# Transposes of attention outputs one list step later and behind the newest matmul

## The chip, the cores and the metric

The kernel runs on one core of a Trainium2 chip. The metric is the device time of one execution in microseconds. Engines are named as in the profile: PE is TensorE's matmuls and PEld its weight loads, DVE is VectorE, ACT is ScalarE, POOL is GpSimd, SP is SyncE, which issues the weight loads from memory.

## The reference

Two transformer blocks of two layers each, on 256 tokens of width 1024 (the second block also carries 256 context tokens in its first layer). Every layer is `h = h + mixer(norm(h)) @ w_out` followed by a gated convolutional feed-forward layer (inner width 2816). The four mixers are the four attentions of the change:

```
layer 1: 8 heads with dilated causal patterns, 8 heads with forget-gate bias, head width 64
layer 2: 8 heads of differential attention, value width 128, RMS norm of each head's output
layer 3: gated linear recurrence, and 8 heads of window attention with a sink column, for the
         256 tokens (keys: context and tokens) and for the context tokens (keys: context)
layer 4: 8 heads of global attention over context and tokens, 8 heads of neighbourhood attention
o = softmax(scores) @ v ;  out = concat(heads) @ w_out ;  h = h + out
```

## The kernel before, in words

All matrix products are split in three: each float32 operand is cut into a high and a low part (`split`, L636), and a product is high x high, high x low and low x high, three matmuls on the same accumulator. Weights come from memory as `raw`, and ScalarE (`wh`) and VectorE (`wl`) cut them (L496, L497).

An attention works on groups of four heads (two pairs; in layer 2 two double heads). For each head the scores are multiplied on TensorE, VectorE finds the extreme and adds the mask, ScalarE takes the exponential, TensorE transposes the probabilities (L810, L820), ScalarE copies them to SBUF, and TensorE multiplies them by the values into the PSUM tile `o`. When a pair of heads is done, `fin_half` (L826) ends it: VectorE inverts the sums and scales `o` into `on` (L832), TensorE transposes the two blocks of 128 tokens of `on` (L836), and `split` cuts the result into `mixh` and `mixl` (L639, L640; `exh`, `exl` in layer 3), which the output projection multiplies. In layer 2 the same is done by `finish` (L1094 to L1110), where the factor comes from a square sum on ScalarE and a power on GpSimd, with the scaling on L1106 and the transposes on L1109. PSUM has two buffers for scores, two for transposes of all kinds, one for `o` and three for projections; `on` has two buffers.

The work is traced as a list of steps. `weave` (L307) spreads a filler list over an attention's list: before entry k of an attention list of length A, the first ceil(k n / A) of n filler steps have been traced. Filler is the next group's projections (12 matmuls a step, or 24), and in the last group of a stage the output projection on the chunks that are ready (`p_out`, 18 matmuls a step in the first, second and last stage, 6 for the last output projection of the third). In layer 1 an attention list has 4 entries (one head each, the second and fourth with the pair's ending inside), in layer 2 6 entries (4 pieces of maps and 2 endings), in layers 3 and 4 10 entries (8 pieces of one head and 128 queries, and 2 endings). The last groups' filler lists have 13 steps (layer 1), 12 (layer 2) and 9 (layer 4); in layer 3 the two groups on the tokens share one filler list of 16. The context attention of layer 3 is woven into the feed-forward layer of layer 2, one entry about every second step.

The order in which each engine gets its instructions is not the traced one. A planner places them by a model of their times: of the instructions whose inputs the model holds ready, an engine gets the one that was traced first. On the chip every engine then works through its own instructions in that fixed order and waits where an input is late. `issue_after(x)` adds one rule to the plan: what is traced inside comes after x on x's engine (in order only; it doesn't wait for x to finish). The kernel before uses it elsewhere, behind weight cuts on VectorE (L589, L1742).

Of the kernel before, what the change touches and what calls it, by code (L numbers as in the profile page):

```python
# [17 lines left out]
S = 256  # L18
# [358 lines left out]
class Prog:  # L377
# [120 lines left out]
            self.W[key] = (h, l)  # L498

    def mm(self, o, a, b, start, stop):  # L500
        self.nc.tensor.matmul(o, a, b, start=start, stop=stop)  # L501

    def mark(self, name):
        def f():
# [318 lines left out]
        for kb in range(nkb):  # L823
            self.mm(o, pts[:, kb], v(kb), kb == 0, kb == nkb - 1)

    def fin_half(self, b, p, h, l):  # L826
        nc = self.nc
        rec = self.small.tile([128, 2, 2], F32, tag="rec", name="rec")
        hs = slice(2 * p, 2 * p + 2)
        nc.vector.reciprocal(rec, b.rs[:, :, hs])  # L830
        on = self.nat.tile([128, 2, 128], F32, tag="on", name="on", bufs=self.bufs[3])
        nc.vector.tensor_tensor(on.rearrange("p a (h d) -> p a h d", d=HD), b.o[:, :, hs],  # L832
                                rec[:, :, :, None].to_broadcast([128, 2, 2, HD]), op=ALU.mult)
        ps = self.ps_t.tile([128, S], F32, tag="t", name="tt")
        for t in range(2):
            nc.tensor.transpose(ps[:, t * 128:(t + 1) * 128], on[:, t], self.ident)  # L836
        self.split(h, l, ps)

    def x_add(self, sts=(), g=None):
        def upd(m, ps):  # L840
# [64 lines left out]
    def plan_attn0(self):  # L905
        boxes = [Box() for _ in range(4)]

        def attend(b, mask, mi, extra=None):
            steps = []

            def head(i):
                if i == 0:
                    b.o = self.ps_o.tile([128, 2, 4, HD], F32, tag="o", name="o")
                    b.rs = self.small.tile([128, 2, 4], F32, tag="rsum", name="rsum")
                p, e = i // 2, i % 2
                P = []
                for qb in range(2):
                    s = self.s_tile()
                    qs, n = slice(qb * 128, (qb + 1) * 128), 128 * (qb + 1)
                    self.qk_s(s[:, :S], (b.q[0][:, e, p, qs], b.q[1][:, e, p, qs]), (b.k[0][:, p], b.k[1][:, p]),  # L920
                              extra(i) if extra else None)
                    P.append(self.soft(s, self.C[mask][:, S - n:], n, b.rs[:, qb, i:i + 1])[0])
                self.causal_pv(P, [b.o[:, 0, i], b.o[:, 1, i]], [b.v[:, kb, i * HD:(i + 1) * HD] for kb in range(2)])
                if i % 2:
                    self.fin_half(b, p, self.mixh[mi][:, p], self.mixl[mi][:, p])
            return [((), lambda i=i: head(i)) for i in range(4)]

        def proj_a(g):
            b = boxes[g]
# [114 lines left out]
    def plan_attn1(self, st, fill, early):  # L1044
# [23 lines left out]
        def attend(g):  # L1068
# [25 lines left out]
            def finish(i):  # L1094
                nc = self.nc
                ss = self.small.tile([128, 2], F32, tag="oss", name="oss")
                v = self.small.tile([128, 2], F32, tag="osv", name="osv")
                rs = b.rs[:, 0, :, i]
                nc.vector.scalar_tensor_tensor(v, rs, 1e-5, rs, op0=ALU.mult, op1=ALU.mult)
                for qb in range(2):  # L1100
                    sq = self.nat.tile([128, 128], F32, tag="osq", name="osq", bufs=2)
                    nc.scalar.activation(sq, b.o[:, qb, i], AF.Square, accum_out=ss[:, qb:qb + 1])
                nc.vector.scalar_tensor_tensor(v, ss, 1.0 / 128, v, op0=ALU.mult, op1=ALU.add)
                r = self.pow_mhalf(v, 2)
                on = self.nat.tile([128, 2, 128], F32, tag="on", name="on", bufs=self.bufs[3])
                nc.vector.tensor_mul(on, b.o[:, :, i], r[:, :, None].to_broadcast([128, 2, 128]))  # L1106
                ps = self.ps_t.tile([128, S], F32, tag="t", name="tt")
                for qb in range(2):
                    nc.tensor.transpose(ps[:, qb * 128:(qb + 1) * 128], on[:, qb], self.ident)  # L1109
                self.split(self.mixh[g][:, i], self.mixl[g][:, i], ps, self.gsub)  # L1110
            for i in range(2):
                for qb in range(2):
                    steps.append(((), lambda i=i, qb=qb: maps(i, qb)))
                steps.append(((), lambda i=i: finish(i)))
            return steps

        self.st1 = self.stat_open(LAT, "sta")
        out = self.p_open("1", first) + fill + proj(0)
# [144 lines left out]
    def plan_even(self, s1, s2):  # L1263
# [83 lines left out]
        def attend(i, lat):  # L1347
# [29 lines left out]
            def finish(p):  # L1377
# [4 lines left out]
                dst = E.sl if lat else E.sc  # L1382
                if p == 0:
                    dst.append(ex([128, 2, S]))
                self.fin_half(b, p, dst[i][0][:, p], dst[i][1][:, p])
            for j in range(4):
                for qb in range(2):
                    steps.append(((), lambda j=j, qb=qb: one(j, qb)))
                if j % 2:
                    steps.append(((), lambda p=j // 2: finish(p)))  # L1390
            return steps

        H = [Box() for _ in range(4)]

# [330 lines left out]
    def plan_odd(self, st):  # L1725
# [51 lines left out]
        def attend(i):  # L1777
            steps, b = [], Q[i]

            def one(j, qb):  # L1780
                nc = self.nc
                if j == 0 and qb == 0:
# [24 lines left out]
            for j in range(4):  # L1807
                for qb in range(2):
                    steps.append(((), lambda j=j, qb=qb: one(j, qb)))
                if j % 2:  # L1810
                    steps.append(((), lambda p=j // 2: self.fin_half(b, p, self.mixh[i][:, p], self.mixl[i][:, p])))
            return steps

        st3 = self.stat_open(LAT, "sta")

# [82 lines left out]
```

## Time and profile before

| | |
|---|---|
| median of 3 runs | 1726.1 us (1724.31 to 1729.87) |
| the profiled execution | 1726.9 us, span 1725.1 us |
| mean granted TensorE clock | 0.981 |
| PE / PEld / DVE / ACT / POOL busy | 97 / 91 / 80 / 55 / 3% of the span |
| instructions | 31957 |

The span goes from the first to the last instruction of the profiled execution. By the tiles in the timeline, the four attention stages lie at about 20 to 131, 335 to 475, 666 to 950 (with the recurrence) and 1300 to 1546 us, the context attention between 475 and 666 us beside a feed-forward layer; the rest is feed-forward layers. A busy time is the union of an engine's instructions; matmuls overlap each other in their modelled lengths, so the start of the next one tells the pace.

### The profile page before, as it was taken

How to read it: one execution, taken by the hardware profiler on the slowest of the kernel's cores; microseconds unless marked ns; L12 is line 12 of the kernel's file. 1: busy time of each engine (PE TensorE's matmuls, PEld its weight loads, DVE VectorE, ACT ScalarE, POOL GpSimd, SP SyncE). 2: the span in 40 equal slices, each digit the busy share in tenths (PEclk: the TensorE clock that was granted, in tenths of full speed). 3: DMA queues.
4: the chain of work that ended last, by engine and by line, in shares of the span. 5: the costliest groups of instructions: out<-in, count | busy, mean ns of one | idle time of the engine just before them, and what ended most of it. 6: DMA issues, size and time to landing. Idle time of an engine off the chain costs nothing.

```text
span 1725.1 us, 31957 instructions
## 1 busy us (share of the span) xinstructions
PE 1670.7 (97%) x12336; PEld 1574.1 (91%) x12336; DVE 1371.5 (80%) x2830; ACT 945.7 (55%) x1687; POOL 59.0 (3%) x75
## 2 busy tenths in 40 slices
PE   7999999999899999999989999999998999999999
PEld 7999999999899999899978988888888998999999
DVE  6798999887787888766786888897779864479887
ACT  6666456656675768444545652342344554466554
POOL 0000000000100000100000000000000220000000
PEclk9999999999999999999989999999998999799999
DMA  8446776554456565334311555655549521135663
GB/s 305 140 142 220 231 219 210 173 173 132 125 173 194 184 206 162 123 124 133 110 62 41 181 182 165 189 169 185 181 150 315 184 62 38 62 121 165 198 191 123
DMA packets 80664, 277.97 MB, mean 161 GB/s; under 512 B 8960, under 2 KB 12160, under 8 KB 80256
## 3 DMA queue, kind: packets, MB, share of 16 engines
q1 hardware_dynamic: 79216, 273.30, 49.6%
q10 hardware_dynamic: 1296, 2.62, 0.4%
q8 instruction: 97, 1.59, 0.4%
q14 instruction: 55, 0.45, 0.1%
HBM read 274.84 MB, written 1.05 MB: 160 GB/s over the span
## 4 chain that ended last, share of the span: by engine, by line
PE 83%; DVE 10%; ACT 4%; issue 2%; DMA 0%; POOL 0%; DVEq 0%; ACTq 0%; POOLq 0%
PE acc L501 55%; PE s L501 20%; PE o L501 4%; DVE wl L497 3%; DVE junk L591 2%; PE ptp L820 2%; ACT wh L496 1%; PE tt L741 1%; DVE x L856 0%; DVE cc L1025 0%; PE stv L501 0%; PE tt L836 0%; DVE nt L1143 0%; ACT L1373 0%; DVE stq L691 0%
## 5 line engine op out<-in xcount | busy, mean ns | idle before, releaser
L496 ACT ACTIVATE wh<-raw 128x1024 fp32r<-128x1024 f32 (+4 forms) x446 | 453.7, 1025 | 453.5 <-PE acc L501 323.6
L497 DVE TENSOR_TENSOR wl<-raw,wh 128x1024 fp32r<-128x1024 f32 (+4 forms) x446 | 524.1, 1180 | 115.1 <-ACT wh L496 113.1
L501 PE MATMUL acc<-nh,wh 128*128 128x256 f32 (+2 forms) x872 | 269.0, 309 | 3.0 <-ACT nh L1145 1.9
L501 PE MATMUL acc<-nh,wl 128*128 128x256 f32 (+2 forms) x872 | 268.7, 308 | 0.5 <-DVE wl L497 0.3
L501 PE MATMUL acc<-nl,wh 128*128 128x256 f32 (+2 forms) x872 | 267.6, 308 | 0.0
L501 PE MATMUL acc<-wh,nh 128*128 128x256 f32 (+2 forms) x768 | 221.9, 290 | 12.4 <-ACT nh L642 7.9
L501 PE MATMUL acc<-wh,nl 128*128 128x256 f32 (+2 forms) x768 | 220.8, 290 | 6.2 <-DVE nl L1146 5.9
L501 PE MATMUL s<-nh,wh 128*128 128x256 f32 (+2 forms) x744 | 223.8, 301 | 2.1 <-ACT sm L1373 1.4
L501 PE MATMUL s<-nh,wl 128*128 128x256 f32 (+2 forms) x744 | 223.7, 301 | 0.0
L501 PE MATMUL s<-nl,wh 128*128 128x256 f32 (+2 forms) x744 | 223.4, 300 | 0.0
L501 PE MATMUL acc<-wl,nh 128*128 128x256 f32 (+2 forms) x768 | 220.8, 288 | 1.6 <-DVE wl L497 1.5
L501 PE MATMUL acc<-g,wh 128*128 128x256 f32 x1056 | 186.2, 279 | 2.7 <-ACT g L639 1.5
L501 PEld LDWEIGHTS acc<-nh,wh 128*128 128x128 f32 x872 | 165.3, 190 | 12.3 <-ACT nh L1145 2.1
L501 PEld LDWEIGHTS acc<-nh,wl 128*128 128x128 f32 x872 | 164.9, 189 | 9.5 <-DVE wl L497 1.2
L501 PEld LDWEIGHTS acc<-nl,wh 128*128 128x128 f32 x872 | 164.8, 189 | 8.6 <-DVE nl L1146 0.2
L591 DVE CUSTOM_DVE_ANT_0 junk<-adaw,sil,c0t 128x1024 f32<-128x1024 f32 x132 | 168.4, 1276 | 0.2
L501 PEld LDWEIGHTS acc<-g,wh 128*128 128x128 f32 x1056 | 160.0, 188 | 4.8 <-ACT g L639 1.9
L501 PEld LDWEIGHTS acc<-wh,nh 128*128 128x128 f32 x768 | 148.8, 194 | 14.7 <-ACT nh L642 8.2
L501 PEld LDWEIGHTS acc<-wh,nl 128*128 128x128 f32 x768 | 148.8, 194 | 8.8 <-DVE nl L1146 7.6
L501 PEld LDWEIGHTS acc<-wl,nh 128*128 128x128 f32 x768 | 148.5, 193 | 3.4 <-DVE wl L497 2.7
L501 PEld LDWEIGHTS s<-nh,wh 128*128 128x128 f32 x744 | 140.1, 188 | 8.4 <-ACT sm L1373 1.6
L501 PEld LDWEIGHTS s<-nl,wh 128*128 128x128 f32 x744 | 139.9, 188 | 6.0
(383 smaller groups left out, 3347.0 us busy)
## 6 DMA issues: line engine op xcount, KB each, us to landing
raw<-in_wts SPq DMA_DIRECT2D x342, 512.0 KB, 4.2
adaw<-in_ada SPq DMA_DIRECT2D x82, 512.0 KB, 4.3
raw<-in_wts SPq DMA_DIRECT2D x72, 448.0 KB, 3.4
raw<-in_wts SPq DMA_DIRECT2D x24, 384.0 KB, 3.2
x<-in_x SPq DMA_DIRECT2D x8, 256.0 KB, 7.1
raw<-in_wts SPq DMA_DIRECT2D x4, 408.0 KB, 3.8
rpb<-in_rpb ACTq DMA_DIRECT2D x1, 1536.0 KB, 6.6
raw<-in_wts SPq DMA_DIRECT2D x2, 528.0 KB, 3.6
```

The source lines that it names most:

```text
L496: nc.scalar.activation(hf[:, c], raw[:, c], AF.Copy)
L497: self.last_wl = nc.vector.tensor_sub(lf[:, c], raw[:, c], hf[:, c].bitcast(F32)).ins
L501: self.nc.tensor.matmul(o, a, b, start=start, stop=stop)
L591: self.nc.vector.tensor_tensor_reduce(out=junk, in0=tiles[j], in1=self.sil[:, c], scale=1.0, scalar=self.C["adab%d" % l][:, m:m + 1], op0= ...
L741: self.nc.tensor.transpose(ps[:, p, t * 128:(t + 1) * 128], src[:, t, p * 128:(p + 1) * 128], self.ident)
L820: self.nc.tensor.transpose(pt[:, kb], P[:, kb * 128:(kb + 1) * 128], self.ident)
```

## The change

`fin_half` and the `finish` of layer 2 end with the scaling into `on`. The transposes and the split move into a new step, `turn_half`, which is a list entry of its own. In layer 1 the entries become heads 0, 1, 2, turn 0, head 3, turn 1; in layer 2 two maps, ending 0, one map, turn 0, one map, ending 1, turn 1; in layers 3 and 4 the turn of the first pair follows the first piece of the third head, and that of the second pair ends the list. Lists grow to 6, 8 and 12 entries. The transposes are traced inside `issue_after(self.last_mm)`: they come after the last matmul that `mm` (L500) has traced by then.

```diff
--- before.py
+++ after.py
@@ -498,7 +498,7 @@
             self.W[key] = (h, l)
 
     def mm(self, o, a, b, start, stop):
-        self.nc.tensor.matmul(o, a, b, start=start, stop=stop)
+        self.last_mm = self.nc.tensor.matmul(o, a, b, start=start, stop=stop).ins
 
     def mark(self, name):
         def f():
@@ -823,7 +823,7 @@
         for kb in range(nkb):
             self.mm(o, pts[:, kb], v(kb), kb == 0, kb == nkb - 1)
 
-    def fin_half(self, b, p, h, l):
+    def fin_half(self, b, p):
         nc = self.nc
         rec = self.small.tile([128, 2, 2], F32, tag="rec", name="rec")
         hs = slice(2 * p, 2 * p + 2)
@@ -831,10 +831,14 @@
         on = self.nat.tile([128, 2, 128], F32, tag="on", name="on", bufs=self.bufs[3])
         nc.vector.tensor_tensor(on.rearrange("p a (h d) -> p a h d", d=HD), b.o[:, :, hs],
                                 rec[:, :, :, None].to_broadcast([128, 2, 2, HD]), op=ALU.mult)
+        b.on = on
+
+    def turn_half(self, b, h, l, scale=None):
         ps = self.ps_t.tile([128, S], F32, tag="t", name="tt")
-        for t in range(2):
-            nc.tensor.transpose(ps[:, t * 128:(t + 1) * 128], on[:, t], self.ident)
-        self.split(h, l, ps)
+        with self.tc.issue_after(self.last_mm):
+            for t in range(2):
+                self.nc.tensor.transpose(ps[:, t * 128:(t + 1) * 128], b.on[:, t], self.ident)
+        self.split(h, l, ps, scale)
 
     def x_add(self, sts=(), g=None):
         def upd(m, ps):
@@ -922,8 +926,13 @@
                     P.append(self.soft(s, self.C[mask][:, S - n:], n, b.rs[:, qb, i:i + 1])[0])
                 self.causal_pv(P, [b.o[:, 0, i], b.o[:, 1, i]], [b.v[:, kb, i * HD:(i + 1) * HD] for kb in range(2)])
                 if i % 2:
-                    self.fin_half(b, p, self.mixh[mi][:, p], self.mixl[mi][:, p])
-            return [((), lambda i=i: head(i)) for i in range(4)]
+                    self.fin_half(b, p)
+
+            def turn(p):
+                self.turn_half(b, self.mixh[mi][:, p], self.mixl[mi][:, p])
+            heads = [((), lambda i=i: head(i)) for i in range(4)]
+            turns = [((), lambda p=p: turn(p)) for p in range(2)]
+            return heads[:3] + turns[:1] + heads[3:] + turns[1:]
 
         def proj_a(g):
             b = boxes[g]
@@ -1104,15 +1113,14 @@
                 r = self.pow_mhalf(v, 2)
                 on = self.nat.tile([128, 2, 128], F32, tag="on", name="on", bufs=self.bufs[3])
                 nc.vector.tensor_mul(on, b.o[:, :, i], r[:, :, None].to_broadcast([128, 2, 128]))
-                ps = self.ps_t.tile([128, S], F32, tag="t", name="tt")
-                for qb in range(2):
-                    nc.tensor.transpose(ps[:, qb * 128:(qb + 1) * 128], on[:, qb], self.ident)
-                self.split(self.mixh[g][:, i], self.mixl[g][:, i], ps, self.gsub)
-            for i in range(2):
-                for qb in range(2):
-                    steps.append(((), lambda i=i, qb=qb: maps(i, qb)))
-                steps.append(((), lambda i=i: finish(i)))
-            return steps
+                b.on = on
+
+            def turn(i):
+                self.turn_half(b, self.mixh[g][:, i], self.mixl[g][:, i], self.gsub)
+            m = [((), lambda i=i, qb=qb: maps(i, qb)) for i in range(2) for qb in range(2)]
+            fin = [((), lambda i=i: finish(i)) for i in range(2)]
+            turns = [((), lambda i=i: turn(i)) for i in range(2)]
+            return m[:2] + fin[:1] + m[2:3] + turns[:1] + m[3:] + fin[1:] + turns[1:]
 
         self.st1 = self.stat_open(LAT, "sta")
         out = self.p_open("1", first) + fill + proj(0)
@@ -1382,13 +1390,19 @@
                 dst = E.sl if lat else E.sc
                 if p == 0:
                     dst.append(ex([128, 2, S]))
-                self.fin_half(b, p, dst[i][0][:, p], dst[i][1][:, p])
+                self.fin_half(b, p)
+
+            def turn(p):
+                dst = E.sl if lat else E.sc
+                self.turn_half(b, dst[i][0][:, p], dst[i][1][:, p])
             for j in range(4):
                 for qb in range(2):
                     steps.append(((), lambda j=j, qb=qb: one(j, qb)))
+                    if j == 2 and qb == 0:
+                        steps.append(((), lambda: turn(0)))
                 if j % 2:
                     steps.append(((), lambda p=j // 2: finish(p)))
-            return steps
+            return steps + [((), lambda: turn(1))]
 
         H = [Box() for _ in range(4)]
 
@@ -1777,6 +1791,9 @@
         def attend(i):
             steps, b = [], Q[i]
 
+            def turn(p):
+                self.turn_half(b, self.mixh[i][:, p], self.mixl[i][:, p])
+
             def one(j, qb):
                 nc = self.nc
                 if j == 0 and qb == 0:
@@ -1807,9 +1824,11 @@
             for j in range(4):
                 for qb in range(2):
                     steps.append(((), lambda j=j, qb=qb: one(j, qb)))
+                    if j == 2 and qb == 0:
+                        steps.append(((), lambda: turn(0)))
                 if j % 2:
-                    steps.append(((), lambda p=j // 2: self.fin_half(b, p, self.mixh[i][:, p], self.mixl[i][:, p])))
-            return steps
+                    steps.append(((), lambda p=j // 2: self.fin_half(b, p)))
+            return steps + [((), lambda: turn(1))]
 
         st3 = self.stat_open(LAT, "sta")
```

## Rows read from the trace of the kernel before

**Rows 1.** The page: busy us, share, count of each engine; chain that ended last.

```profile
PE 1670.7 (97%) x12336; PEld 1574.1 (91%) x12336; DVE 1371.5 (80%) x2830; ACT 945.7 (55%) x1687; POOL 59.0 (3%) x75
...
PE 83%; DVE 10%; ACT 4%; issue 2%; DMA 0%; POOL 0%; DVEq 0%; ACTq 0%; POOLq 0%
```

**Rows 2.** Stages: window, length, busy us (count) by engine, PEclk, DMA, GB/s.

```profile
335.00:475.00 140.00, 133.83 (x1114) 131.54 (x1114) 111.63 (x285) 86.15 (x198) 11.32 (x12) 0.99 0.47 144
...
1300.00:1546.00 246.00, 234.12 (x1775) 222.57 (x1774) 162.93 (x336) 128.20 (x242) 26.00 (x21) 0.93 0.37 121
```

**Rows 3.** TensorE's waits: line, what ended it, us in total, times, longest.

```profile
PE tt L836 <- DVE on L832: 3.9, 7, 0.9
...
PE tt L1109 <- DVE on L1106: 3.8, 3, 1.9
...
PE acc L501 <- ACT mixh L639: 0.9, 2, 0.5
...
PE acc L501 <- ACT mixh L642: 0.8, 2, 0.6
...
PE tt L836 <- DVE msink L1374: 0.5, 1, 0.5
```

**Rows 4.** Tiles on and tt: instruction, count, ns min/median/max, first and last start.

```profile
L836 PE MATMUL tt<-c0t,on x48: 270/273/474, 58.4 to 1525.6; 128*128 128x128 f32 x48
...
L832 DVE TENSOR_TENSOR on<-o,rec x24: 408/424/426, 55.2 to 1524.9; 128x256 f32<-128x256 f32 x24
...
L1106 DVE TENSOR_TENSOR on<-o,rs x8: 415/424/425, 381.8 to 467.5; 128x256 f32<-128x256 f32 x8
...
L639 ACT ACTIVATE mixh<-tt x16: 362/383/392, 59.7 to 1525.9; 128x256 fp32r<-128x256 f32 x16
...
L640 DVE TENSOR_TENSOR mixl<-tt,mixh x16: 410/420/425, 60.5 to 1526.3; 128x256 fp32r<-128x256 f32 x16
```

**Rows 5.** TensorE's timeline, mid-stage: start us, length us, instruction, [idle before, releaser].

```profile
118.49 0.44 PE L836 MATMUL tt<-c0t,on 128*128 128x128 f32 x2 [0.46 <-DVE on L832]
...
439.77 0.44 PE L1109 MATMUL tt<-c0t,on 128*128 128x128 f32 x2 [1.50 <-DVE on L1106]
...
445.50 0.44 PE L1109 MATMUL tt<-c0t,on 128*128 128x128 f32 x2 [0.39 <-DVE on L1106]
...
540.04 0.44 PE L836 MATMUL tt<-c0t,on 128*128 128x128 f32 x2 [0.89 <-DVE on L832]
...
908.16 0.44 PE L836 MATMUL tt<-c0t,on 128*128 128x128 f32 x2 [0.52 <-DVE msink L1374]
...
1453.62 0.44 PE L836 MATMUL tt<-c0t,on 128*128 128x128 f32 x2 [0.52 <-DVE on L832]
```

**Rows 6.** Busy time of the engines around the wait at 118.49 us.

```profile
118.00:122.00 4.00, 3.39 (x28) 3.11 (x28) 4.00 (x14) 1.87 (x7) 0.00 (x0) 1.00 0.30 119
```

**Rows 7.** TensorE's timeline, waits at the ends of stages.

```profile
138.83 0.44 PE L836 MATMUL tt<-c0t,on 128*128 128x128 f32 x2 [0.52 <-DVE on L832]
...
139.74 0.61 PE L501 MATMUL acc<-mixh,wh 128*128 128x256 f32 x3 [0.47 <-ACT mixh L639]
...
468.12 0.41 PE L1109 MATMUL tt<-c0t,on 128*128 128x128 f32 x2 [1.94 <-DVE on L1106]
...
939.59 0.44 PE L836 MATMUL tt<-c0t,on 128*128 128x128 f32 x2 [0.52 <-DVE on L832]
...
1525.41 0.44 PE L836 MATMUL tt<-c0t,on 128*128 128x128 f32 x2 [0.52 <-DVE on L832]
...
1526.32 0.63 PE L501 MATMUL acc<-mixh,wh 128*128 128x256 f32 x3 [0.47 <-ACT mixh L639]
```

**Rows 8.** Chain in order of time: start us, length us; one feed-forward step.

```profile
1550.13 2.88 PE s L501 x24
```

**Rows 9.** Windows before and in the stretch at half clock, last attention stage.

```profile
1450.00:1460.00 10.00, 7.65 (x56) 6.38 (x55) 4.77 (x12) 4.07 (x10) 1.64 (x1) 1.00 0.14 41
...
1460.00:1484.00 24.00, 24.00 (x106) 21.59 (x106) 9.03 (x24) 9.24 (x21) 0.00 (x0) 0.50 0.00 1
```

## The prediction

> **What bounds the kernel now.** I read the page's engine table first. TensorE is busy 97% of the span [rows 1], and the chain of work that ended last lies on it for 83% [rows 1]. Its idle time is 1725.1 - 1670.7 = 54.4 us, and a change that leaves the instructions alone can only win from that, or from time at the lower clock. The windows by stage show where it lies: 6.2 us in the second attention stage and 11.9 us in the last one, where the clock is below full as well [rows 2]. Then the waits of TensorE say how much of it belongs to the moved instructions: 3.9 + 0.5 us in front of the transposes of L836, and 3.8 us in front of those of L1109, together 8.2 us in 11 waits, for 32 pairs of transposes. Waits for what these transposes feed (mixh) are small, 0.9 + 0.8 us [rows 3]. So 8.2 us, 0.47% of the span, is the most that the edit can win at the waits themselves.
>
> **What moves and what it costs.** No instruction is added or removed. The 24 + 8 scalings on VectorE (0.42 us each), the 48 + 16 transposes (0.27 us each as modelled), and the copies that follow on ScalarE (0.38 us) and VectorE (0.42 us) stay [rows 4]. They issue no DMA. The weight loads on SyncE's queue keep their order, since each is issued by the filler step that needs it, and the filler lists are not reordered; GpSimd's one operation per half in the second stage (the power) stays in the finishing step. What changes is (a) TensorE's place for each pair of transposes, behind the last matmul traced before it, and (b) the weaving: every attention's list gets two more entries (six for four in the first stage, eight for six in the second, twelve for ten in the others), so each entry is followed by a smaller share of filler.
>
> (a) *Waits in mid-stage.* Seven waits have work behind them: 0.46, 1.50, 0.39, 0.89 and 0.52 us, and two of 0.52 us at 1453.62 and 1488.59 us [rows 5]. While a transpose waits, everything queued behind it on TensorE waits. At 540.04 us the next matmuls are down projections of the feed-forward layer, which depend on nothing in the attention: with the 24 matmuls of a feed-forward step (2.88 us [rows 8]) ahead of the transposes, the 0.42 us scaling is over long before. I take the whole 0.89. At 908.16 us score matmuls follow: the whole 0.52. At 1453.62 us other transposes follow, then matmuls that need results not there yet: half, and the same at 1488.59, so 0.52 for the two. At 118.49 us VectorE is busy all 4.00 of 4.00 us [rows 6], so a wait filled there comes back as a wait for VectorE: half, 0.23. At 439.77 and 445.50 us the score buffers are full and the projections already issued, so the newest matmul may lie in front of the transposes already and the edge changes nothing: half, 0.75 + 0.20. Sum 3.11 us; the bounds are 0 and 4.80.
>
> (b) *Stage ends.* Four waits lie at ends of stages, where no filler is left: 0.52, 1.94, 0.52 and 0.52 us, and behind two of them 0.47 us more for the copy [rows 7]. A later place can't fill these; only an earlier start of the last head can. By the weaving rule the filler steps issued before the last head go from 10 to 9 of 13 in the first stage, stay at 8 of 12 in the second, go from 15 to 14 of 16 in the third and from 8 to 7 of 9 in the last. One step is 18 matmuls, 18 x 2.88/24 = 2.2 us [rows 8], in the third 6, 0.7 us. That covers the end of the first stage (0.99 us; half taken, since VectorE is full there), of the third (0.52) and part of the last (0.52: there all 9 filler steps still precede the last transposes, so nothing covers the copy). The 1.94 us of the second stage, the largest, stays. Sum 1.54 us; bounds 0 and 3.5 + 0.94 = 4.44.
>
> (c) *What comes late next.* The copy of a transposed pair now lands later, and output projections that need it may wait. The waits for mixh of today are 1.7 us [rows 3]; I add half, 0.85 us; bounds 0 and the rival below. A transposed pair holds one of two buffers it shares with the heads' transposes for 0.38 + 0.42 us as before, only at another time; nothing for that, at worst one such hold per wait, which is inside the range.
>
> **Sum.** -3.11 - 1.54 + 0.85 = -3.8 us. The profiled execution took 1726.9 us (span 1725.1 and 1.8 us around it), so 1723.1 by it; it lies 0.8 us above the median of 1726.1, so 1722.3 us as the measurement will show it. Bounds of the terms: -4.80 - 4.44 = -9.2 us on one side, the +11.0 us of the late outputs below on the other.
>
> **A rule weighed.** Five of the waits are the same 0.52 us: 138.83, 939.59, 1453.62, 1488.59 and 1525.41 [rows 5, 7]. The trace names VectorE's scaling as what ended each, and its 0.42 us [rows 4] fits into 0.52: a chain, not a lack of room. If these five stay for whatever reason, the sum loses the 0.50 + 0.52 + 0.52 + 0.52 us taken for them and ends at -1.7 us, 1724.4 us; that is a rival of its own, "the repeated gap". The Trainium skill (Perfetto Trace Analysis, Optimization Strategy) says that one gap repeating on the engine that should be full can mean too few SBUF or PSUM buffers. By it none of these five would move with the transposes' place. The trace speaks against it: the releaser is an instruction that writes data, not one that frees a buffer.
>
> **Rivals.**
> *Nothing moves.* The order on each engine is a plan. Where the newest traced matmul is issued before the scaling ends, the edge holds nothing back and the transposes stay where they were. For it: at 439.77 and 468.12 us TensorE had run out of filler. Against it: at 540.04 and 908.16 us it had not [rows 5]. Then only 0.89 + 0.52 us go and 0.85 come: 1726.1 - 0.6 = 1725.5 us.
>
> *Outputs too late (the slower side).* In the three stages with an output projection in the weave, the third and the fourth attention's last chunk are wanted by the very next projection steps, in the third stage the last one: 7 places. If the transposes stand behind one projection step there, 2.2 us each, TensorE runs out of ready work, as it does today at 139.74 us for 0.47 us [rows 7]. Two such places cancel the gain (4.4 against 3.8); with five it is 11.0 - 3.8 = +7.2, 1733.3 us. For it: the mixh waits exist, and in the last stage all filler precedes the last transposes. Against it: it needs five of seven places without other ready work, and on today's trace the rows name mixh for four waits of 0.4 us on average [rows 3].
>
> *The clock.* From 1460 to 1484 us TensorE is busy 24.00 of 24 us at a granted clock of 0.50, which is 1.2 of 2.4 GHz, while VectorE is busy 9.03 and ScalarE 9.24; in the ten us before it TensorE was busy 7.65 [rows 9], with the 0.52 us wait among its gaps. At full clock its work would take some 12 us. If the new order keeps TensorE fuller before 1460, part of that comes back: between 0 and 12 us; VectorE's 9.03 and ScalarE's 9.24 us in one chain with it keep it from all, so I take 8: 1722.3 - 8 = 1714.3 us. The same mechanism can take: a new stretch at 0.50 as long as one row above costs half its length. The Trainium skill (Perfetto Trace Analysis, Matmul Optimizations) says the matmul engine scales its power with use, so matmuls should run back to back; the two rows agree in direction.
>
> **Chances.** Forecast (some waits filled, 1718 to 1726) 0.43; the clock 0.23; outputs too late 0.20; nothing moves 0.10; the repeated gap 0.04. A measurement of this kernel can tell about 0.3% or 5.2 us from no change, so faster means under 1720.9 us and slower over 1731.3. Faster: 0.18 of the forecast's 0.43 and all of the clock's, 0.41. Slower: the late outputs, 0.20, and 0.01 of a plan that comes out worse elsewhere. Same: the rest, 0.38. The range for 8 in 10 goes to the clock's and the late outputs' times with a little beyond on the first side, since that stretch can give up to 12: 1710 to 1733. Cases of both signs hold much of it, so the forecast's own range, 1718 to 1726, stands beside it.
>
> **What would show it.** Right: the waits of TensorE in front of the two transpose lines fall from 8.2 to about 4 us, those at 540 and 908 us gone, the 1.94 us at the end of the second attention stage still there; mixh waits up by a microsecond or less; busy times and counts of each engine unchanged. Wrong: transposes' waits near 8 us (nothing moved), mixh waits of 5 us and more (outputs late), or a granted clock in the last attention stage that leaves 0.93 by more than 0.02 (the clock decides). It would also be wrong if the largest difference lay in a stage without attention, or in VectorE's or ScalarE's order.

## The result and the profile after

The changed kernel takes 1735.33 us (median of 6 runs, 1729.51 to 1737.44) against 1725.07 us for the kernel before in the same runs: a ratio of 1.0056 [1.0034, 1.0077]. It is slower, by some 9.7 us by the ratio (10.3 by the medians); the forecast was 1722.3 us. Single executions of one kernel differ with the granted clock (those of the kernel before lie between 1718.4 us at a mean clock of 0.987 and 1732.3 us at 0.978, one of 5737.6 us left out), so a trace shows one case and the runs' medians and ratios decide.

First the page of the changed kernel, engines and chain [rows 1], then its windows over the second attention stage and the last one (moved by 8 us) [rows 2].

```profile
PE 1672.7 (96%) x12336; PEld 1575.5 (91%) x12336; DVE 1371.0 (79%) x2830; ACT 950.8 (55%) x1689; POOL 58.1 (3%) x75
...
PE 83%; DVE 10%; ACT 4%; issue 2%; DMA 1%; POOL 0%; DVEq 0%; ACTq 0%; POOLq 0%; SPq 0%
```

```profile
335.00:475.00 140.00, 132.73 (x1095) 130.43 (x1094) 109.12 (x280) 84.23 (x192) 10.57 (x12) 0.98 0.46 144
1308.00:1554.00 246.00, 234.89 (x1783) 224.05 (x1782) 162.39 (x335) 128.44 (x242) 25.40 (x21) 0.92 0.37 121
```

The same bound and the same work, with ScalarE 5 us busier and two instructions more on it. TensorE's waits in the changed kernel (line, what ended it, us in total, times, longest) answer to [rows 3]:

```profile
PE o L501 <- ACT pt L646: 3.5, 3, 2.1
...
PE tt L840 <- DVE on L832: 2.7, 4, 1.2
PE ptp L820 <- ACT sm L1381: 2.7, 2, 1.9
...
PE tt L840 <- DVE on L1115: 2.3, 1, 2.3
...
PE acc L501 <- ACT mixh L642: 1.9, 2, 1.4
...
PE acc L501 <- ACT mixh L639: 0.5, 1, 0.5
```

The waits in front of the moved transposes fell from 8.2 us [rows 3] to 2.7 + 2.3 = 5.0, as forecast; those for mixh went from 1.7 to 2.4. The new ones stand above them: 3.5 us for copied probabilities and 2.7 us for exponentials. In all, TensorE is idle for 1733.4 - 1672.7 = 60.7 us, against 54.4 before.

Where the 8.3 us of the two profiled executions went is seen when both are cut at the same point of the work, the start of the 211th low cut of weights (L497), behind the context attention. Windows of the kernel before, then of the changed one:

```profile
0.00:678.20 678.20, 653.76 (x5515) 644.80 (x5516) 565.72 (x1186) 434.44 (x792) 18.18 (x35) 0.99 0.58 186
678.20:1725.10 1046.90, 1016.97 (x6824) 929.26 (x6822) 805.82 (x1646) 511.25 (x895) 40.79 (x40) 0.97 0.46 145
```

```profile
0.00:686.60 686.60, 657.08 (x5509) 648.05 (x5510) 565.64 (x1187) 439.48 (x798) 17.67 (x35) 0.99 0.57 184
686.60:1733.40 1046.80, 1015.64 (x6830) 927.42 (x6828) 805.37 (x1644) 511.33 (x892) 40.45 (x40) 0.98 0.45 145
```

All of it lies ahead of the cut: 8.4 us, 5.1 as idle TensorE (29.52 against 24.44 us) and 3.3 as more busy time for the same work. The second part goes with the clock: the stretches at a granted clock of 0.50 add up to 20.5 us there, against 6.8. The low cuts show no loss up to the 404th us, 0.3 us at 490, 5.1 at 550, 8.8 at 589; neighbouring cuts scatter by 2 to 4 us around such a figure, as each plan places them anew. So the loss begins at the end of the second attention and is made beside the context attention, in the feed-forward layer of layer 2, where the prediction had looked for one wait of 0.89 us. TensorE's waits there, 476 to 672 us, before and after:

```profile
PE s L501 <- ACT sm L1373: 1.4, 1, 1.4
PE tt L836 <- DVE on L832: 0.9, 1, 0.9
PE ptp L820 <- ACT sm L1373: 0.6, 1, 0.6
```

```profile
PE o L501 <- ACT pt L646: 3.5, 3, 2.1
PE ptp L820 <- ACT sm L1381: 2.7, 2, 1.9
```

The wait at the transposes is gone, and waits of the heads' own chain (exponential, copy of the probabilities) have come.

### The profile page after: what moved, and what is told of

It reads as the page before. It is cut to its first block, busy times and chain, and to the rows that moved or that the text cites. A ratio compares the mean times of both kernels' runs of the same rounds, so it can differ in the third digit from the quotient of the medians.

```text
span 1733.4 us, 31966 instructions
## 1 busy us (share of the span) xinstructions
PE 1672.7 (96%) x12336; PEld 1575.5 (91%) x12336; DVE 1371.0 (79%) x2830; ACT 950.8 (55%) x1689; POOL 58.1 (3%) x75
## 4 chain that ended last, share of the span: by engine, by line
PE 83%; DVE 10%; ACT 4%; issue 2%; DMA 1%; POOL 0%; DVEq 0%; ACTq 0%; POOLq 0%; SPq 0%
PE acc L501 54%; PE s L501 20%; PE o L501 5%; DVE wl L497 3%; PE ptp L820 2%; ACT wh L496 1%; DVE junk L591 1%; DVE x L860 1%; PE tt L741 1%; ACT L1036 1%; DVE nt L1151 1%; PE stv L501 1%; PE tt L840 0%; DVE stq L691 0%; DMA raw<-in_wts 0%
## 5 line engine op out<-in xcount | busy, mean ns | idle before, releaser
L497 DVE TENSOR_TENSOR wl<-raw,wh 128x1024 fp32r<-128x1024 f32 (+4 forms) x446 | 525.1, 1182 | 105.9 <-ACT wh L496 103.7
L501 PE MATMUL acc<-wh,nh 128*128 128x256 f32 (+2 forms) x768 | 220.7, 288 | 12.6 <-ACT nh L642 7.9
```

The lines of the kernel that those rows point to most:

```text
L497: self.last_wl = nc.vector.tensor_sub(lf[:, c], raw[:, c], hf[:, c].bitcast(F32)).ins
L501: self.last_mm = self.nc.tensor.matmul(o, a, b, start=start, stop=stop).ins
```

## The experiments

Three theories stood first: A, the context attention beside the feed-forward layer makes the loss; B, the edge (the order that `issue_after` sets) makes it; C, the other spacing loses some in every stage. "Context" is layer 3's attention for the context tokens, "latent" its attention for the 256 tokens; `pin=False` in a diff means without the edge. Each kernel was timed against the kernel before in its own runs (medians of it 1724.9 to 1726.9 us). Losses in us below are the ratio's, times 1726; intervals are 95%.

| run | kernel | median us | ratio |
|---|---|---|---|
| e1 | changed, context attention as before | 1731.8 | 1.0042 [1.0028, 1.0055] |
| e2 | before, two empty entries in each context list | 1730.0 | 1.0025 [1.0009, 1.0041] |
| e3 | changed, no edge | 1734.9 | 1.0059 [1.0044, 1.0073] |
| e4 | changed, sink exponential beside the softmax | 1733.4 | 1.0048 [1.0032, 1.0064] |
| e5 | change in the context attention alone | 1726.9 | 1.0012 [0.9997, 1.0027] |
| e6 | change in the first two attentions alone | 1729.6 | 1.0020 [1.0006, 1.0033] |
| e7 | change in the latent and last attentions alone | 1727.6 | 1.0017 [1.0000, 1.0033] |
| e8 | changed, no entry more | 1726.4 | 1.0004 [0.9988, 1.0019] |
| e9 | before, two empty entries in every list | 1736.4 | 1.0070 [1.0044, 1.0095] |
| e10 | both pairs a step later, no entry more | 1709.3 | 0.9914 [0.9896, 0.9931] |
| e11 | before, endings merged: fewer entries | 1734.9 | 1.0064 [1.0045, 1.0082] |
| e12 | e10's form in the last attention alone | 1714.3 | 0.9927 [0.9909, 0.9946] |
| e13 | e10's form in all but the last | 1726.6 | 1.0003 [0.9990, 1.0017] |
| e14 | e10 without the edge | 1709.8 | 0.9908 [0.9890, 0.9925] |
| e15 | one pair of the last attention | 1726.5 | 0.9986 [0.9968, 1.0003] |
| e16 | e12 with two empty entries in each of its lists | 1715.4 | 0.9938 [0.9917, 0.9958] |
| e17 | e12, second pairs only | 1727.6 | 1.0011 [0.9995, 1.0026] |
| e18 | changed, last attention as in e12 | 1722.1 | 0.9978 [0.9963, 0.9993] |

**e1 to e4: which part of the change, in the place where the loss is seen.** e1 gives the context attention its 10 entries and its transposes their old place:

```diff
+                if not lat:
+                    self.turn_half(b, dst[i][0][:, p], dst[i][1][:, p], pin=False)
...
-                    if j == 2 and qb == 0:
+                    if lat and j == 2 and qb == 0:
...
-            return steps + [((), lambda: turn(1))]
+            return steps + ([((), lambda: turn(1))] if lat else [])
```

> The change everywhere except in the context attention woven into the feed-forward layer of layer 2, which keeps its list of 10 entries with the transposes inside the ending and no edge. In the trace of the changed kernel all of the 8.3 us lie between 490 and 660 us, so theory A (the loss is the context attention's list among the feed-forward steps) expects 1725 to 1727 us, and no wait of TensorE over 1.5 us for 'sm' or 'pt' between 490 and 660 us. Theory B (the transposes behind the newest matmul cost in all four attentions) expects 1732 us or more. Theory C (any new plan lands somewhere within 10 us, tied to no part) expects nothing in particular; 1732 or more would fit it too.

e2 does only the spacing there, on the kernel before:

```diff
+                    if not lat and j == 2 and qb == 0:
+                        steps.append(((), lambda: None))
...
-            return steps
+            return steps + ([] if lat else [((), lambda: None)])
```

> The kernel before with two empty entries in each context attention's list, at the places where the change puts its turns; no transpose moves. If the loss comes from the spacing (34 for 30 entries over the feed-forward steps) and not from the move of the transposes, 1731 to 1737 us. If it comes from the move or from the edge, 1724 to 1727 us, as before. The plan of this kernel has 41 activation table loads on ScalarE against 37 before and 39 in the changed one: if these loads carry the loss, 4 more x 1.28 us with the waits they bring give 1730 or more.

e3 takes the edge away:

```diff
-        with self.tc.issue_after(self.last_mm):
-            for t in range(2):
-                self.nc.tensor.transpose(ps[:, t * 128:(t + 1) * 128], b.on[:, t], self.ident)
+        for t in range(2):
+            self.nc.tensor.transpose(ps[:, t * 128:(t + 1) * 128], b.on[:, t], self.ident)
```

> The changed kernel with its new entries but without the rule that queues the transposes behind the newest matmul. Theory A (spacing of the context attention's list) expects 1733 to 1737 us, as changed. Theory B (the edge holds the transposes back and what needs them waits) expects 1724 to 1728 us.

e4 puts the sink's exponential right behind that of the softmax, head by head, where the changed kernel takes it for two heads in the ending:

```diff
-                nc.vector.tensor_sub(b.ms[:, qb, j:j + 1], m, si)
+                nc.scalar.activation(b.ms[:, qb, j:j + 1], si, AF.Exp, bias=m, scale=-1.0)
...
-                nc.scalar.activation(b.ms[:, :, hs], b.ms[:, :, hs], AF.Exp)
```

> The changed kernel, where the exponential of the sink column is taken right behind each softmax exponential of layer 3 (8 small ones per group in place of 2, and VectorE's subtraction before it is gone), so ScalarE needs no switch of its table for it alone. Two table loads for that line stand in the changed kernel's trace, and the waits of TensorE at 538.4 us (1.13 us) and 587.9 us (2.09 us, followed by 3.4 us at half clock) come right behind them. If the separated sink exponentials are what makes TensorE wait, about 1.1 + 2.1 + 1.7 = 5 us go: 1729 to 1731 us. If the order of the pieces alone does it, 1734 to 1737 us.

e3 equals the changed kernel: the edge neither costs nor gains, theory B falls. e1 leaves 7.2 of 9.7 us, so the context attention isn't all. e2 moves no transpose and loses 4.3 us, less than expected but clear of zero: the entries by themselves cost something. e4 was aimed at a chain that the changed kernel's ScalarE shows (first fence) ahead of TensorE's largest new wait (second):

```profile
582.19 1.28 ACT L1036 ACT_TABLE_LOAD   x1
583.49 0.42 ACT L1036 ACTIVATE cc<-cc 128x256 f32<-128x256 f32 x1
583.92 1.28 ACT L1388 ACT_TABLE_LOAD   x1
585.22 0.21 ACT L1388 ACTIVATE msink<-msink 128x4 f32<-128x4 f32 x1
...
587.53 0.36 ACT L646 ACTIVATE pt<-ptp 128x256 f32<-128x256 f32 x1
```

```profile
587.94 1.11 PE L501 MATMUL o<-vs,pt 128*128 128x64 f32 x4 [2.09 <-ACT pt L646]
```

The feed-forward's activation (L1036) and the exponentials want different tables, and each change is a load of 1.28 us. The Trainium skill (ScalarE: Activation LUTs, Table sets: the hidden batching unit) has the rule to batch calls by table set; the trace shows why here, as the sink's exponential costs a load of its own between two of the other set. By e4, though, a plan without these two loads gains 1.4 us, within the intervals. Its trace says why it is so little: the two waits aimed at, 1.13 us at 538.4 us and 2.09 us at 587.9 us, are gone or down to 0.65 us, and TensorE is idle 57.0 us instead of 60.7, but the mean granted clock is 0.977 instead of 0.979, which is 78.5 us at 0.50 instead of 71.7. And e2 and e5 have 41 loads, four more than before, at a loss of 4.3 and 2.1 us, so the number of loads doesn't give the time.

**e5 to e8: which stage, and the move or the entries.** e5 to e7 are the changed kernel with the code of e1's kind in all other attentions (`fin_half` followed by the unpinned `turn_half` in one entry). e8 has all moves and edges, with the turns inside their neighbours' entries (its lines for the last attention; the others likewise):

```diff
-                    if j == 2 and qb == 0:
-                        steps.append(((), lambda: turn(0)))
+                    steps.append(((), lambda j=j, qb=qb: (one(j, qb), turn(0) if (j, qb) == (2, 0) else None)))
...
-                    steps.append(((), lambda p=j // 2: self.fin_half(b, p)))
-            return steps + [((), lambda: turn(1))]
+                    steps.append(((), lambda p=j // 2: (self.fin_half(b, p), turn(1) if p else None)))
+            return steps
```

> The kernel before, with the change in the context attention of the third stage alone (its lists get 12 entries, its transposes the edge); the other three attentions as before. Theory A (the loss is made by the context attention in the feed-forward stage, 490 to 660 us): most of the change's +10 us by the medians comes with this kernel, 1731 to 1735 us, and its trace lags by 6 us or more from 660 us on. Theory C (every re-spaced stage loses some, in shares that add): it gives what the change loses over the kernel with the old context list, 1735.3 - 1731.8 = +3.5, so 1727 to 1731 us. A rival, that nothing adds up and each new order lands anywhere within some 5 us: any of these, with lags that jump in stages whose code isn't changed.

> The kernel before, with the change in the first two attentions alone (up to about 505 us). Theory A: no change, 1723 to 1727 us. Theory C: part of the +6.9 us which the kernel with the old context list kept; its trace lost 3.3 us between 404 and 535 us, so 1727 to 1730 us, and the lag of its trace is reached by 535 us and stays. The prediction's own terms for these two stages (a gain of some 2 us) would give 1723 us.

> The kernel before, with the change in the latent attention of the third stage and the attentions of the last one alone. Theory A: no change, 1723 to 1727 us. Theory C: the rest of the +6.9 us, 1727 to 1730 us, with no lag before 850 us and most of it after 1450 us, in a longer stretch at half clock (30.7 us where the kernel before has 24). The prediction's terms for these stages (a gain of some 2 us, and a shorter half-clock stretch as its best case) would give 1715 to 1723 us.

> The kernel after, but no list gets an entry more: the transposes of a first pair are issued within the entry that they followed, those of a last pair within the entry that scales, all with the edge. So the transposes' place stays moved for the first pairs and the filler is spaced as before. Theory S (the loss comes from the spacing that the two more entries bring): 1720 to 1727 us, at or below the kernel before, since the waits in mid-stage are still filled. Theory T (the moved transposes make what follows late): 1731 to 1736 us, as after.

The parts lose 2.1, 3.5 and 2.9 us by their ratios, 8.5 together for 9.7: theory A falls, and the sum speaks for a spread loss (C), although of the three only e6 is clear of zero by itself (the interval of e5 holds 1, that of e7 begins at it). The prediction's gains for single stages aren't seen in any of them. e8 costs nothing that can be told (+0.7 us), so entries, not late transposes, are what costs. But e8 moves only first pairs really (a second pair behind the newest matmul of its own entry stands where it did), and its waits at the transposes are 4.2 + 3.5 = 7.7 us.

**e9 to e11: entries alone, both pairs without entries, fewer entries.** e9 is e2's edit in all four attentions. e11 runs each ending within the last head's entry (lists of 4, 8 and 8 for 6, 10 and 10). e10 has e8's first pairs, and hands a second pair to the first entry of the next list of the same attention; lists keep their lengths (the new lines for the last attention):

```diff
+    def defer(self, later, f):
+        if later:
+            self.pend = f
+        else:
+            f()
...
+    def late(self):
+        f, self.pend = getattr(self, "pend", None), None
+        if f:
+            f()
...
+                    steps.append(((), lambda j=j, qb=qb: (one(j, qb), turn(0) if (j, qb) == (2, 0) else self.late() if (j, qb) == (0, 0) else None)))
...
+                    steps.append(((), lambda p=j // 2: (self.fin_half(b, p), self.defer(i < 3, lambda: turn(1)) if p else None)))
```

> The kernel before, transposes where they were and no edge, with two empty entries in every list of all four attentions, where the changed kernel has its transposes' entries. Theory S (the entries' spacing of the filler makes the loss, the moved transposes win back a part): about the time of after or above it, 1733 to 1738 us, with TensorE idle for 58 us or more, transposes' waits among it near 8 us. Theory T (the transposes' lateness makes it): 1723 to 1728 us.

> The transposes of a first pair within the entry that they followed, those of a second pair within the first entry of the next list of the same attention (the last list's at once), all with the edge: both pairs come a step later, and no list gets an entry. Theory S: the transposes' waits fall from 8.2 to 4 or 5 us as in after, and nothing is paid for it: 1719 to 1724 us, faster than both kernels by 1 to 4 us. Theory T: the second pairs, which the output projections want soonest, come late again: 1729 to 1736 us. A rival, that these waits are never worth their length because what follows them waits a little later: 1724 to 1728 us, with the transposes' waits down to 5 us and TensorE's idle time still at 53 to 55 us.

> The kernel before with fewer entries: the finishing step of a pair of heads runs within the entry of the last head instead of in one of its own (4 entries for 6 in the second attention, 8 for 10 in the third and the last; the first has none to merge). The transposes keep their place right behind the scaling. Theory S1 (more filler behind each entry covers the attention's own waits, so fewer entries are better): 1718 to 1723 us, and TensorE idle for less than 53 us. Theory S2 (the plan before is one of the better of many that scatter by some us, and any other spacing costs): 1727 to 1735 us, TensorE idle for 56 us or more.

e9 decides it: without one moved transpose the entries cost 12 us by the ratio (1.0070), the whole loss and a little more. Its windows, cut at the same point, and its waits at the transposes:

```profile
0.00:688.30 688.30, 655.87 (x5509) 646.23 (x5510) 567.35 (x1187) 440.40 (x798) 18.30 (x35) 0.99 0.54 183
```

```profile
PE tt L1111 <- DVE on L1108: 5.6, 2, 3.3
...
PE tt L836 <- DVE on L832: 3.2, 5, 1.1
```

Ahead of the cut it lost 10.1 us (idle 32.43, 8.0 more than before) and nothing behind it. Beside the context attention, 476 to 672 us, it has the changed kernel's new waits, though no transpose moved:

```profile
PE o L501 <- ACT pt L646: 3.3, 2, 2.2
PE ptp L820 <- ACT sm L1377: 2.7, 2, 1.9
```

The changed kernel has 2.9 us less idle time ahead of the cut and 5.0 instead of 8.8 us at the transposes: by these two traces that is what the move gave back. By the ratios it is 2.4 us, with intervals that overlap. e11 says that it isn't a matter of more or fewer: fewer entries cost 11 us too, with idle time of 54.4 us before and 1736.4 - 1677.5 = 58.9 in it. S2 of the two theories stands: the spacing before is better than both neighbours that were tried. Why a spacing is worse, beyond the waits shown, the runs don't tell.

e10 was to win 1 to 4 us and won 15. Its page, and its windows at the same cut:

```profile
PE 1650.4 (97%) x12336; PEld 1556.7 (91%) x12336; DVE 1370.2 (80%) x2830; ACT 944.0 (55%) x1685; POOL 57.7 (3%) x75
```

```profile
0.00:678.50 678.50, 652.31 (x5517) 644.86 (x5518) 566.88 (x1186) 432.68 (x790) 18.25 (x35) 0.99 0.55 186
678.50:1706.40 1027.90, 998.09 (x6822) 911.81 (x6820) 803.29 (x1646) 511.33 (x895) 39.43 (x40) 0.99 0.44 147
```

19.0 us come from behind the cut (1046.9 to 1027.9), and 18.9 of them are busy time of TensorE: the same work at a higher clock. Its idle time, 1706.5 - 1650.4 = 56.1 us, is no less than the 54.4 before.

**e12 to e15: which place holds those 15 us.** e12 and e13 are e10's edit in the last attention alone and in all others; e14 is e3's edit on e10; e15 defers one pair, the second list's second in the last attention:

```diff
+                    steps.append(((), lambda p=j // 2: (self.fin_half(b, p), self.defer(True, lambda: turn(1, True)) if (i, p) == (1, 1) else turn(p))))
```

> The kernel before, with the last attention alone in the form that gave 1709.3 us in all four (first pairs within the entry that they followed, second pairs within the next list's first entry, edge kept, 10 entries). Theory L (the gain is the stretch at half clock behind the boundary of the second and third list, some 24 us that need 12, and the gaps ahead of it): 1710 to 1715 us, and no stretch at half clock over 4 us between 1400 and 1540 us. Theory M (the gain is spread over the four attentions, each some 4 us): 1720 to 1723 us, the stretch still there.

> The complement: that form in the first three stages' attentions, the last attention as before. Theory L: 1721 to 1727 us, with some 24 us at half clock from 1455 us on. Theory M: 1711 to 1716 us.

> The version of 1709.3 us without the edge behind the newest matmul. As the edge was worth nothing in the changed kernel (1734.9 without it, 1735.3 with it), 1708 to 1711 us. If the edge keeps the planner from putting the transposes ahead of the first scores of the next list, where they would wait for VectorE: 1716 us or more, the waits at the transposes back at 7 us or more.

> The kernel before, with one pair of transposes moved: that of the second list's second pair of heads in the last attention, into the third list's first entry, with the edge. It is the pair that TensorE waits 0.52 us for at 1453.62 us in the kernel before, 6 us ahead of the 24 us at half clock. Theory L in its narrow form (this pair delays the third list's start): 1710 to 1716 us, no half-clock stretch there. If the earlier start of the third list comes from more than this pair (the first pairs too, or the places in the lists): 1723 to 1727 us, with the 0.52 us gone and the stretch still there.

Theory L holds: the last attention alone gives 12.6 us, the others nothing, the edge nothing, and the one pair nothing that can be told. What differs stands in TensorE's timeline at the boundary of the second and third list. The wait there in the kernel before; then the changed kernel, then e12:

```profile
1459.03 0.66 PE L820 MATMUL ptp<-c0t,sm 128*128 128x128 f32 x4 [1.44 <-ACT sm L1804]
```

```profile
1459.70 0.38 PE L840 MATMUL tt<-c0t,on 128*128 128x128 f32 x2
1459.92 0.60 PE L741 MATMUL tt<-c0t,qn 128*128 128x128 f32 x4
...
1461.30 0.38 PE L501 MATMUL s<-nk0h,qlh 64*128 64x256 f32 x1 [0.36 <-ACT qlh L642]
...
1463.34 0.28 PE L501 MATMUL s<-nk1h,qll 64*128 64x256 f32 x1
1465.40 1.11 PE L820 MATMUL ptp<-c0t,sm 128*128 128x128 f32 x4 [1.78 <-ACT sm L1821]
```

```profile
1452.66 0.61 PE L741 MATMUL tt<-c0t,qn 128*128 128x128 f32 x4
...
1454.05 0.38 PE L501 MATMUL s<-nk0h,qlh 64*128 64x256 f32 x1 [0.43 <-ACT qlh L642]
...
1455.97 0.39 PE L501 MATMUL acc<-mixh,wh 128*128 128x256 f32 x1
...
1457.02 0.28 PE L501 MATMUL acc<-mixh,wl 128*128 128x256 f32 x1
1458.30 0.66 PE L820 MATMUL ptp<-c0t,sm 128*128 128x128 f32 x4 [1.00 <-ACT sm L1827]
...
1461.44 0.39 PE L851 MATMUL tt<-c0t,on 128*128 128x128 f32 x2
```

In the changed kernel the outputs' transposes go first, then those of the next list's queries and its scores; the output projection's matmuls are spent by then, and TensorE waits 1.78 us for the first exponential. In e12 the query goes first, nine matmuls of the output projection (1455.97 to 1457.02) lie between the scores and the transposes that need the exponential, the wait is 1.00 us, and the outputs' transposes come at 1461.44. What follows differs more than the wait. The changed kernel's windows, then e12's:

```profile
1460.00:1470.00 10.00, 7.82 (x38) 6.03 (x37) 4.39 (x13) 3.94 (x9) 1.64 (x1) 0.75 0.15 43
1470.00:1480.00 10.00, 10.00 (x46) 9.22 (x44) 4.51 (x12) 3.27 (x8) 0.00 (x0) 0.50 0.00 0
```

```profile
1450.00:1460.00 10.00, 8.52 (x67) 7.61 (x66) 6.03 (x14) 5.43 (x10) 1.64 (x1) 1.00 0.29 81
1460.00:1470.00 10.00, 10.00 (x80) 8.94 (x80) 6.16 (x18) 6.29 (x14) 0.00 (x0) 1.00 0.01 2
```

From the longer wait on (the record falls at 1465.04 us, within it) the granted clock is 0.50 (1.2 of 2.4 GHz) for 27.3 us, with 46 matmuls in 10 us; behind the shorter one it stays at 1.00, with 80. The stretch is that of [rows 9].

**e16 to e18: entries or place in the last attention, and the sum.** e16 adds empty entries to e12 (first diff), e17 puts e12's first pairs back behind their scaling (second), e18 is the changed kernel with e12's lines in its last attention:

```diff
+                    if j == 2 and qb == 0:
+                        steps.append(((), lambda: None))
...
-            return steps
+            return steps + [((), lambda: None)]
```

```diff
-                    steps.append(((), lambda j=j, qb=qb: (one(j, qb), turn(0) if (j, qb) == (2, 0) else self.late() if (j, qb) == (0, 0) else None)))
+                    steps.append(((), lambda j=j, qb=qb: (one(j, qb), self.late() if (j, qb) == (0, 0) else None)))
...
-                    steps.append(((), lambda p=j // 2: (self.fin_half(b, p), self.defer(i < 3, lambda: turn(1)) if p else None)))
+                    steps.append(((), lambda p=j // 2: (self.fin_half(b, p), self.defer(i < 3, lambda: turn(1)) if p else turn(0, False))))
```

> The kernel with only the last attention in the form of next-list's first entry (1714.3 us), with two empty entries in each of that attention's lists, where the change has its transposes' entries. If the entries' spacing is what keeps the change from this gain: 1723 to 1729 us, with 20 us or more at half clock between 1450 and 1500 us. If it is where the transposes stand: 1711 to 1717 us, no such stretch.

> The same kernel of 1714.3 us, with the first pairs' transposes back right behind their scaling, so that only the second pairs of the first three lists of the last attention are moved. The second pairs stand at the boundaries of the lists, ahead of the next list's first scores. If they make the gain: 1711 to 1717 us. If it needs the first pairs too (as the one pair alone, 1726.5 us, makes possible): 1722 to 1728 us, with the stretch at half clock still there.

> The changed kernel with its last attention in that form (10 entries, second pairs in the next list's first entry), the other three as changed. If the stages add up: 1735.3 less the 12.6 us, 1720 to 1725 us; the loss between 460 and 660 us is still in its trace. If the gain needs the order that the kernel before has in the earlier stages: 1728 us or more.

In the last attention the entries cost nothing that can be told (e16) and the place is all: a second pair at the end of its own list (e7) wins nothing, in the next list's first entry it wins 12 us. It takes both pairs: in e17 the nine matmuls are issued ahead of the scores and the wait is 1.78 us again; e8, with the first pairs alone, has 1.79. The two effects add up: e18 takes 13.3 us off the changed kernel's median, and its trace still has the loss ahead of the cut (the cut lies at 685.8 us, against 678.2 before).

## Why the prediction was wrong

*(a) Mid-stage waits, -3.11.* Right in kind, and larger than taken. Of the seven waits, 4.80 us [rows 5], one of 0.52 us is left, at 1496.39 us: -4.28. That at 439.77 us went, but one of 1.81 us for the query's transposes came at 443.34.

*(b) Stage ends, -1.54.* Wrong in sign. The four waits of 3.50 us [rows 7] are 1.18, 2.35, 0.52 and 0.52 us now, 4.57. No earlier start of the last heads shows in them. It is right that the 1.94 us of the second stage stay (2.35).

*(c) Late outputs, +0.85.* Right: the waits for mixh grew by 0.7 us, from 1.7 [rows 3]. The rival of the late outputs gave 1733.3 us, near the measured time, by a mechanism that isn't there: no place lost 2.2 us to mixh, and e9 loses as much with the transposes where they were.

*The step that failed* is part (b) of what moves: "every attention's list gets two more entries ... so each entry is followed by a smaller share of filler". It was priced only as an earlier start of the last heads, inside the -1.54 us. That all heads lie closer together, and the whole plan is another one, had no term; e9 measures it at 12 us. So no row of waits at the moved instructions could have given the answer: every sign of being right that the prediction names for the waits came true (8.2 us down to 5.0, those at 540 and 908 us gone, the one at the end of the second attention still there, mixh up by less than a microsecond), and the kernel was slower all the same. The prediction's last condition, the largest difference in a stage without attention, comes near (the place is a feed-forward layer, with the context attention woven in), but it had no price.

*The clock* (0.23, 1714.3 us) named the right stretch and a size near the right one: e12 wins 12.6 us there, where 8 were taken. But the order of the changed kernel doesn't shorten the longest of the gaps ahead of it, the wait for the first exponential (1.44 us before, 1.78 after); the 0.52 us that the prediction saw there wasn't the one (e15 is without it and has 27.3 us at 0.50). The stage's granted clock went from 0.93 to 0.92.

*Nothing moves* and *the repeated gap* fall: the transposes moved, and of the five gaps of 0.52 us one became 1.18, one went and three stayed.

## What to carry to other kernels

An edit that adds an entry to a woven list is two edits: price the new spacing of everything else by itself, with empty entries, before crediting the move. A wait that goes isn't time that is won: here 3.2 us less at the transposes came with 6.3 us more idle time in all. The place to look for more is the gap that stands ahead of a stretch at half clock, and what could be issued inside it. The version to use here is e10: 1709.3 us, 0.9914 [0.9896, 0.9931] of the kernel before.

## What the runs showed of the hardware

At the boundary of the second and third list of the last attention, every trace with a wait of 1.44 us (before) or of 1.78 or 1.79 us (the changed kernel, e1 to e9, e11, e13, e15, e17) has a stretch at a granted clock of 0.50, although TensorE was busy 10.00 of 10 us in it (shown above for the changed kernel): 24 to 31 us in most, 20.5 us in e9, 13.7 us in e2 and e13. Behind waits of 0.98 to 1.00 us (e12, e16, e18) and where there was none (e10, e14) there was no such stretch. So the order there, a few tenths of a microsecond of gaps, goes with over 12 us.

That it is the one wait, and not the whole order around it, is not shown; no run changed the wait alone. Two readings speak against the wait alone: the same 1.79 us stood ahead of 13.7 us (e13) and of 30.7 us (e7), and the recorded clock fell 1.2 us behind the end of the wait in the kernel before (1460.22 us), within it in the changed kernel (1465.04 us), and as it began in e7 (1453.52 us). That gaps go with a lower clock was in the prediction; that it stays down so long under a full TensorE, and that so little saves it, was not.
